# Second FFN down stage: seven half-size products per batch of blocks in place of eight, with six running sums on chip

## The chip, the cores and the metric

The kernel runs on one core of one Trainium2 chip. The metric is the device time of one execution in microseconds (us). A time from a profile is from one profiled execution; its span goes from the first to the last instruction.

The engines are called as in the profile: PE is TensorE (matmul), PEld its weight loads, DVE is VectorE, ACT is ScalarE, POOL is GpSimd, and SP is SyncE, which here only issues DMAs.

## The reference

One layer of a hybrid encoder: chunked attention and an RWKV-7 time mix, gated and merged, and then a feed-forward part. All is float32. The change touches only the second matrix product of the feed-forward part and what follows it:

```python
D_MODEL = 1024; SEQ = 2048; D_FF = 4096
...
hf = rms_norm(x, pre_ffn_g[l])
u = jnp.square(jax.nn.relu(hf @ w_up[l])) @ w_down[l]
x = x + rms_norm(u, post_ffn_g[l])
```

The stage in question computes `u` and the last line for the upper half of the sequence, 1024 tokens: a product of 1024 x 4096 by 4096 x 1024.

## The kernel before

**Precision.** Every float32 product is made of three passes on TensorE. `split` writes an operand as a high part (a cast on ScalarE to the matmul's float32 format, line 66) and a low part (source minus high part on VectorE, line 67). `mm3` (line 75) then issues high x high, high x low and low x high into the same PSUM tile.

**Order of the program.** `run` goes through four groups of 512 tokens (RWKV, attention, merge), and then through the feed-forward part in two halves of 1024 tokens: `phase_up(0)`, `phase_down(0)`, `phase_up(1)`, `phase_down(1)`. Beside `phase_down(0)` other work is interleaved; beside `phase_down(1)` there is none. The tile framework allots the buffers, sets the semaphores and orders the instructions of each engine beforehand.

**The up stage** writes the hidden activations, transposed, to DRAM: `self.ad[fb]` holds block `fb` of 128 hidden features, as 128 partitions x 2 groups x 512 tokens. There are 32 such blocks for a half. It uses the same kind of seven-product scheme already, for the first product of the feed-forward part.

**The down stage before** (`phase_down`) takes two blocks at a time. `load(fb)` fetches 128 rows of `w_down` (512 KB, `wdraw`) and the block of activations (512 KB, `araw`) through SP's queue into two of the four `raw` buffers, and splits both into a tile `fop` of 16 KB a partition; the tiles come in turn from the pool of `z` (two buffers) and a ring of two. `down` runs the products of the two blocks and adds each PSUM tile to the sums `u` of eight token tiles by 1024 columns (line 1178):

```python
for t in range(th * GT, (th + 1) * GT):
    for n in range(2):
        ps = pn.tile([P, G], F32, tag="dn", name="ps_dn")
        self.mm3(ps, [(w[:, 2, sl], w[:, 3, sl], w[:, 0, ns], w[:, 1, ns]) for w in ws])
        ...
        nc.vector.tensor_tensor(u[t][:, ns], u[t][:, ns], ps, ALU.add)
```

`pn` has four PSUM buffers. So each output tile of 128 tokens by 512 columns takes six matmuls and one eviction for each pair of blocks.

**The end.** In the last pair of blocks, `final(th)` follows the four token tiles of a group: two squares with a sum on ScalarE (line 1188), three small GpSimd operations that make the reciprocal root `r` (lines 1191, 99, 101), a product with the gain on VectorE (line 1193), two scaled adds with the residual `x1r` (line 1196) and the DMA to the output (line 1199). The closing work of the first group runs beside the products of the second.

**Memory.** The pools of the up stage (`ht`, `up`, `ops`) stand on the left of the on-chip memory, those of the down stage partly on the right in the same place. A tile that reuses memory waits for the last user of the tile that was there. `raw` (four buffers of 4 KB a partition), `z` (two of 16 KB), the pool `b` (tags `bh` and `bl`, 16 KB each) and PSUM stay allotted over both stages.

Of the kernel before, what the change touches and what calls it, by code (L numbers as in the profile page):

```python
# [8 lines left out]
F32 = mybir.dt.float32  # L9
BF16 = mybir.dt.bfloat16  # L10
F32R = mybir.dt.float32r
AF = mybir.ActivationFunctionType
ALU = mybir.AluOpType
# [4 lines left out]
P = 128  # L18
D = 1024
KB = D // P  # L20
FF = 4096
HW = 512
NP = 4
G = 512
GT = G // P
# [3 lines left out]
RMS_EPS = 1e-6  # L29
# [12 lines left out]
def advance(steps, n=None):  # L42

    while n is None or n > 0:
        if next(steps, steps) is steps:
            return
        n = n and n - 1


class Block:  # L50
# [1091 lines left out]
    def phase_down(self, half, zp, rp, cb, pn, beside_of):  # L1142
# [4 lines left out]
        with ExitStack() as ctx:  # L1147
# [63 lines left out]
                        advance(beside, 1)  # L1211
            advance(beside)


    def run(self):
        tc, e = self.tc, None
        with ExitStack() as ctx, ExitStack() as mixing:
            e = mixing.enter_context
            consts = self.constants(ctx, mixing)
            advance(consts, 1)  # L1220
            self.pd = ctx.enter_context(tc.tile_pool(name="pd", bufs=2, space=PSUM))
            self.wp = e(tc.tile_pool(name="w", bufs=2))
            self.hp = e(tc.tile_pool(name="h", bufs=1))
            with tc.tile_pool(name="p0", bufs=2, reuse_waits="tile") as sp, \
                 tc.tile_pool(name="p0p", bufs=2, space=PSUM, reuse_waits="tile") as pt:
                advance(self.phase_norm(0, sp, pt, GT))
            advance(consts)
            self.order, self.next = [], None
            for g in range(self.NG):
                self.g = g  # L1230
                self.phase_rwkv(g)
                self.phase_attention(g)
                with ExitStack() as c:
                    early = iter(())
                    if g == self.NG - 1:
                        early = self.combinations(0, c.enter_context(tc.tile_pool(name="p1", bufs=1, reuse_waits="tile")), 2)
                    sp = c.enter_context(tc.tile_pool(name="p0", bufs=2, reuse_waits="tile"))
                    pt = c.enter_context(tc.tile_pool(name="p0p", bufs=2, space=PSUM, reuse_waits="tile"))
                    o = [sp.tile([P, D], F32, tag="o", bufs=GT, name=f"o{t}") for t in range(GT)]
                    self.phase_merge(g, o, self.after(g, sp, pt), early)  # L1240
                    for t in range(GT):
                        self.nc.scalar.dma_start(self.od[g][t], o[t])
            mixing.close()
            e = ctx.enter_context
            zp = e(tc.tile_pool(name="z", bufs=2, reuse_waits="tile"))
            bp = e(tc.tile_pool(name="b", bufs=1, reuse_waits="tile"))
            rp = e(tc.tile_pool(name="raw", bufs=4, side="right", reuse_waits="tile"))
            cb = e(tc.tile_pool(name="cb", bufs=3, side="right", reuse_waits="tile"))
            pn = e(tc.tile_pool(name="ffpd", bufs=4, space=PSUM, reuse_waits="tile"))

            def beside(op, pt):
                for g in (2, 3):
                    yield from self.residuals(g, op, pt, 1)
                yield from self.combinations(1, op)
                yield from self.first_half(2, bp)

            advance(self.first_half(0, bp))
            self.phase_up(0, zp, rp, cb, pn, 8)
            self.phase_down(0, zp, rp, cb, pn, beside)
            self.phase_up(1, zp, rp, cb, pn, 8)  # L1260
            self.phase_down(1, zp, rp, cb, pn, lambda op, pt: iter(()))


_INS = [
# [35 lines left out]
```

## Time and profile before

| what | value |
|---|---|
| median of 3 runs | 3430.61 us (3426.16 to 3436.8) |
| the profiled execution | 3436.05 us |
| its span | 3434.4 us |
| mean granted TensorE clock | 0.988 |
| busy: PE, DVE, ACT, POOL | 96%, 70%, 41%, 12% of the span |
| 3120 to 3200 us: PE, DVE, ACT, POOL busy | 80.00, 53.12, 12.90, 0.00 us |
| 3120 to 3200 us: DMA | 0.29 of 16 engines, 92 GB/s |

A row of the timeline gives start and duration in us, engine, line, operation, output <- inputs, shapes and the number of instructions merged (x2); where an engine sat idle before it, the idle time and what ended it stand in brackets. A row of the groups gives the sum of the busy time and the mean in ns, and then the idle time of the engine just before them. A row of windows gives, for each engine, busy time and instructions in a stretch, then the granted clock, the DMA share and GB/s. A row of the chain gives start, time, engine and line of one link of the work that ended last.

### The profile page before, as it was taken

To read this page: it belongs to the slowest core of one execution; us is meant where nothing else is said; L and a number is where in the kernel's file an instruction comes from. 1 tells how busy PE (TensorE), PEld (TensorE's weight loads), DVE (VectorE), ACT (ScalarE), POOL (GpSimd) and SP (SyncE) were. 2 spreads that over 40 slices of the span, in tenths; PEclk is the share of its full clock that TensorE was granted. 3 is DMA by queue.
4 is the path that set the end of the run, shared out by engine and by line. 5 is a ranking of instruction groups with operands and counts; after the bars stand their busy time and mean duration, and the time that the engine had idled before them with its cause. 6 is when DMAs were issued, how large, how long until landed. Compare 5 with 4: busy or idle time off the path is not lost. (4 is left out here: it accounts for less than half of the span.)

```text
span 3434.4 us, 50373 instructions
## 1 busy us (share of the span) xinstructions
PE 3297.5 (96%) x19233; PEld 2674.4 (78%) x19233; DVE 2412.8 (70%) x4110; ACT 1414.1 (41%) x2319; POOL 419.6 (12%) x796
## 2 busy tenths in 40 slices
PE   7999999999989999989999989999999999999998
PEld 5777777777867777867777877888888878888886
DVE  5774856766865766865775865877887788676667
ACT  4434634436644435644445634333321243331112
POOL 2210002101022111012210000111200021100001
PEclk9999999999999999999999999999999999999999
DMA  5224353225373125373224276434845374343333
GB/s 146 84 82 130 130 191 113 63 90 191 113 270 123 59 87 181 120 264 123 72 88 143 90 267 217 132 117 148 297 152 182 95 241 135 117 144 98 98 98 110
DMA packets 397864, 481.10 MB, mean 140 GB/s; under 512 B 17516, under 2 KB 304432, under 8 KB 397624
## 3 DMA queue, kind: packets, MB, share of 16 engines
q1 hardware_dynamic: 346168, 364.63, 34.1%
q0 software_dynamic: 23040, 79.71, 6.1%
q10 hardware_dynamic: 28416, 33.56, 2.9%
q8 instruction: 151, 2.47, 0.3%
q14 instruction: 89, 0.73, 0.1%
HBM read 356.16 MB, written 124.81 MB: 140 GB/s over the span
## 5 line engine op out<-in xcount | busy, mean ns | idle before, releaser
L75 PE MATMUL ps_dn<-fop 128*128 128x512 f32 x3072 | 702.6, 390 | 4.1 <-DVE u L1178 4.1
L75 PEld LDWEIGHTS ps_dn<-fop 128*128 128x128 f32 x3072 | 576.7, 188 | 126.2 <-DVE u L1178 6.0
L75 PE MATMUL psd<-hh,whi 128*128 128x512 f32 x1344 | 542.8, 404 | 8.0 <-ACT whi L66 7.1
L75 PE MATMUL psd<-hl,whi 128*128 128x512 f32 x1344 | 541.7, 403 | 0.0
L75 PE MATMUL psd<-hh,wlo 128*128 128x512 f32 x1344 | 538.4, 401 | 0.6 <-DVE wlo L67 0.5
L66 ACT CAST whi<-wraw 128x1024 fp32r<-128x1024 f32 x232 | 243.2, 1049 | 516.9 <-PE psd L75 405.8
L1178 DVE TENSOR_TENSOR u<-u,ps_dn 128x512 f32<-128x512 f32 x480 | 323.3, 685 | 149.5 <-PE ps_dn L75 148.7
L67 DVE TENSOR_TENSOR wlo<-wraw,whi 128x1024 fp32r<-128x1024 f32 x232 | 282.9, 1220 | 199.1 <-ACT whi L66 180.9
L75 PEld LDWEIGHTS psd<-hh,whi 128*128 128x128 f32 x1344 | 256.9, 191 | 60.9 <-ACT whi L66 7.9
L75 PEld LDWEIGHTS psd<-hh,wlo 128*128 128x128 f32 x1344 | 256.5, 191 | 50.5 <-DVE wlo L67 2.0
L75 PEld LDWEIGHTS psd<-hl,whi 128*128 128x128 f32 x1344 | 256.8, 191 | 50.0
L66 ACT CAST fop<-wdraw 128x1024 fp32r<-128x1024 f32 x64 | 67.0, 1047 | 427.4 <-PE ps_dn L75 236.0
L1099 POOL DMA_DIRECT2D ad<-r x128 | 69.2, 541 | 586.3 <-DVE r L1098 570.2
L968 PE MATMUL ps_o<-whi,mh 128*128 128x512 f32 x256 | 103.4, 411 | 16.6 <-ACT whi L66 12.3
L75 PE MATMUL ps_p<-yh,whi 128*128 128x512 f32 x256 | 103.8, 405 | 14.6 <-DVE th L939 12.7
L66 ACT CAST s12h<-s 128x1024 fp32r<-128x1024 f32 x32 | 33.7, 1054 | 184.6 <-PE ps_u L75 184.6
L831 DVE CUSTOM_DVE_ANT_0 sc<-bias,ps_s 128x640 f32<-128x640 f32 (+4 forms) x128 | 93.4, 730 | 22.3 <-PE ps_pt L843 18.1
L836 ACT ACTIVATE sc<-sc,mn 128x640 f32<-128x640 f32 (+4 forms) x128 | 97.7, 764 | 19.3 <-DVE mn L831 18.5
L75 PE MATMUL ps_p<-yh,wlo 128*128 128x512 f32 x256 | 104.2, 408 | 0.1
L847 ACT CAST PTh<-ps_pt 128x640 fp32r<-128x640 f32 (+4 forms) x128 | 80.0, 625 | 58.7 <-PE ps_pt L843 57.6
L75 PE MATMUL ps_p<-yl,whi 128*128 128x512 f32 x256 | 103.5, 404 | 0.0
L1097 ACT ACTIVATE r<-r 128x512 f32<-128x512 f32 x128 | 80.7, 630 | 54.2 <-DVE r L1096 54.0
(352 smaller groups left out, 6668.2 us busy)
## 6 DMA issues: line engine op xcount, KB each, us to landing
wraw<-in_w_in_dram SPq DMA_DIRECT2D x168, 512.0 KB
wraw<-in_w_up_dram SPq DMA_DIRECT2D x80, 512.0 KB
ad<-r POOLq DMA_DIRECT2D x128, 256.0 KB, 2.4
wdraw<-in_w_down_dram SPq DMA_DIRECT2D x64, 512.0 KB
araw<-ad SPq DMA_DIRECT2D x64, 512.0 KB
gd<-gate ACTq DMA_DIRECT2D x64, 256.0 KB
th<-gd SPq DMA_DIRECT2D x32, 512.0 KB
wraw<-in_w_out_dram SPq DMA_DIRECT2D x32, 512.0 KB
```

Of the source, the lines that this page charges most:

```text
L66: self.nc.scalar.copy(hi, src)
L67: self.nc.vector.tensor_tensor(lo, src, hi.bitcast(F32), ALU.subtract)
L75: mm = nc.tensor.matmul(ps, l, r, start=n == 0, stop=n == last).ins
L831: nc.vector.tensor_tensor_reduce(sc[:, 0:n], bias[:, s0:640], pss[:, c0 : c0 + n], 1.0, 3.0e38, ALU.add, ALU.min, mn,)
L836: nc.scalar.activation(sc[:, 0:n], sc[:, 0:n], AF.Exp, scale=-1.0, bias=mn, accum_out=sm)
L847: nc.scalar.copy(hv, pst[:, 0:nk])
L968: nc.tensor.matmul(ps[t], l[:, k, ts], r[:, k % 2], start=k == 0 and j == 0, stop=k == KB - 1 and j == 2)
L1097: nc.scalar.activation(r, r, AF.Relu)
L1099: nc.gpsimd.dma_start(self.ad[fb][:, th], r)
L1178: nc.vector.tensor_tensor(u[t][:, ns], u[t][:, ns], ps, ALU.add)
```

## The change

The second call of `phase_down` is replaced by a new function, `phase_down_fast`. The rest of the kernel stays.

**The products.** The 1024 x 4096 by 4096 x 1024 product is taken as 16 pairs of blocks. With the tokens in two groups, the columns in two halves, and the two blocks of a pair as the inner halves, it is a product of 2 x 2 quarters: a11, a12, a21, a22 by b11, b12, b21, b22. Seven products of combined quarters make the four output quarters in place of eight: the operands of step 1 are a11 and b11, of step 2 a12 and b21, of step 3 a sum of quarters `s` and b22, of step 4 a22 and a sum `t`, of steps 5 and 6 earlier values of `s` and `t`, and of step 7 the differences a11 - a21 and b22 - b12.

**Batches.** The 16 pairs go in batches of 2, 4, 4, 4 and 2. Within a batch a product of step `m` sums over all its pairs in PSUM: 4 token tiles of 128, each 3 matmuls a pair. Its tiles are then added to running sums that live through all batches: four output quarters `y`, and `xs` and `v7`, which several outputs share. In the first batch the sums begin with a copy on ScalarE where they are new; in the last batch `xs` and `v7` are added to the outputs, and `final(th, t)` follows each tile of steps 2 and 4. The order of the steps is 5, 6, 3, 4, 7, 1, 2, with other orders in the first and the last batch.

**Operands.** `operands(b, m)` makes the combinations of a step, on VectorE for `t` in steps 5 and 6 and on GpSimd for the others, in pieces of 128 x 1024, and splits both operands piece by piece. It is called for the next step before `product` of the present one. In a full batch a step takes one `z` buffer and one of `bh` and `bl`; in a batch of two a step takes one of these four.

**Loads.** Eight quarters have one buffer each, 8 KB a partition, on the right side (`fdq`). `fetch` loads quarters of the next batch after the step that used the present ones last; `free` lists which ones after which step. A piece of an activation quarter comes by two DMAs of 256 KB, a piece of a weight quarter by one of 512 KB, all by SP. The first batch has its first four quarters in the `raw` buffers and the others in halves of four of the eight buffers; from the second batch on, `s` and `t` take the `raw` buffers.

The diff, without its empty lines:

```diff
--- before.py
+++ after.py
@@ -1211,6 +1211,202 @@
                         advance(beside, 1)
             advance(beside)
 
+    def phase_down_fast(self, half, zp, bp, rp, cb, pn):
+        tc, nc, a = self.tc, self.nc, self.a
+        H = D // 2
+        gs = (2 * half, 2 * half + 1)
+        batches, at = [], 0
+        for x in (2, 4, 4, 4, 2):
+            batches.append((at, x))
+            at += x
+        assert at == FF // P // 2
+        end = len(batches) - 1
+        order = [(5, 6, 3, 4, 7, 1, 2)] * len(batches)
+        order[0], order[end] = (2, 1, 5, 6, 7, 4, 3), (5, 6, 3, 1, 2, 7, 4)
+        factors = {1: ("a11", "b11"), 2: ("a12", "b21"), 3: ("s", "b22"), 4: ("a22", "t"),
+                   5: ("s", "t"), 6: ("s", "t"), 7: ("a21", "b12")}
+        free = [{7: ("a11",), 4: ("b21",), 3: ("b22", "a12")}]
+        free += [{4: ("a22",), 7: ("a21", "b12", "b22"), 1: ("b11", "a11"), 2: ("a12", "b21")}] * end
+        with ExitStack() as ctx:
+            e = ctx.enter_context
+            cp = e(tc.tile_pool(name="fdu", bufs=1, reuse_waits="tile"))
+            qp = e(tc.tile_pool(name="fdq", bufs=1, side="right", reuse_waits="tile"))
+            y = [cp.tile([P, GT, D], F32, name=f"y{i}") for i in range(2)]
+            xs = cp.tile([P, GT, H], F32, name="xs")
+            v7 = cp.tile([P, GT, H], F32, name="v7")
+            lo, hi = slice(0, H), slice(H, D)
+            Q = {}
+            def quarter(tag):
+                return qp.tile([P, 4, H], F32, tag=tag, name="q" + tag)
+            def pair():
+                return rp.tile([P, D], F32, tag="raw", name="wdraw").rearrange("p (i n) -> p i n", i=2)
+            def load(b, q, pieces):
+                i0, x = batches[b]
+                r, c = int(q[1]) - 1, int(q[2]) - 1
+                Q[b, q] = pieces
+                for j, t in enumerate(pieces):
+                    i = i0 + 2 * j
+                    if q[0] == "a":
+                        for k in range(2):
+                            nc.sync.dma_start(t[:, k], self.ad[2 * (i + k) + c][:, r])
+                    else:
+                        rows = a["w_down"][2 * i * P : (2 * i + 4) * P, c * H : (c + 1) * H]
+                        nc.sync.dma_start(t, rows.rearrange("(i c p) n -> c p i n", c=2, p=P)[r])
+            def fetch(b, qs):
+                for q in qs:
+                    t = quarter(q)
+                    load(b, q, [t[:, j : j + 2] for j in range(0, batches[b][1], 2)])
+            for q in ("a12", "b21", "a11", "b11"):
+                load(0, q, [pair()])
+            home = {q: quarter(q) for q in ("a12", "b21", "a11", "b22")}
+            for q, t in (("a22", "a12"), ("a21", "b21"), ("b12", "a11"), ("b22", "b22")):
+                load(0, q, [home[t][:, 0:2]])
+            Q[0, "s"], Q[0, "t"] = [home["a12"][:, 2:4]], [home["b21"][:, 2:4]]
+            fetch(1, ("a21", "a22", "b12", "b11"))
+            def combine(eng, b, o, x, op, z):
+                for t, u, v in zip(Q[b, o], Q[b, x], Q[b, z]):
+                    eng.tensor_tensor(t, u, v, op)
+            made = []
+            def operands(b, m):
+                x = batches[b][1]
+                if (b, "s") not in Q:
+                    Q[b, "s"], Q[b, "t"] = ([pair() for _ in range(0, x, 2)] for _ in range(2))
+                if m == 5:
+                    combine(nc.gpsimd, b, "s", "a21", ALU.add, "a22")
+                    combine(nc.vector, b, "t", "b12", ALU.subtract, "b11")
+                elif m == 6:
+                    combine(nc.gpsimd, b, "s", "s", ALU.subtract, "a11")
+                    combine(nc.vector, b, "t", "b22", ALU.subtract, "t")
+                elif m == 7:
+                    combine(nc.gpsimd, b, "a21", "a11", ALU.subtract, "a21")
+                    combine(nc.gpsimd, b, "b12", "b22", ALU.subtract, "b12")
+                i = len(made)
+                if x == 4:
+                    t = [zp.tile([P, 4, D], F32R, tag="z", name="fop").rearrange("p f (i n) -> p (f i) n", i=2),
+                         bp.tile([P, KB, G], F32R, tag="b" + "hl"[i % 2], name="fop2")]
+                elif i % 4 < 2:
+                    t = [zp.tile([P, 4, D], F32R, tag="z", name="fop").rearrange("p f (i n) -> p (f i) n", i=2)]
+                else:
+                    t = [bp.tile([P, KB, G], F32R, tag="b" + "hl"[i % 2], name="fop2")]
+                f = []
+                for n, q in enumerate(factors[m]):
+                    dst = t[n] if x == 4 else t[0][:, 4 * n : 4 * n + 4]
+                    h, l = dst[:, 0:x], dst[:, x : 2 * x]
+                    f.append((h, l))
+                for j in range(0, x, 2):
+                    for (h, l), q in zip(f, factors[m]):
+                        self.split(h[:, j : j + 2], l[:, j : j + 2], Q[b, q][j // 2])
+                if m == 6:
+                    combine(nc.gpsimd, b, "s", "a12", ALU.subtract, "s")
+                    combine(nc.gpsimd, b, "t", "b21", ALU.subtract, "t")
+                made.append(f)
+            def keep(dst, ps, new):
+                if new:
+                    nc.scalar.copy(dst, ps)
+                else:
+                    nc.vector.tensor_tensor(dst, dst, ps, ALU.add)
+            def product(b, m, f):
+                x = batches[b][1]
+                (ah, al), (bh, bl) = f
+                add = lambda o, z: nc.vector.tensor_tensor(o, o, z, ALU.add)
+                for t in range(GT):
+                    ts = slice(t * P, (t + 1) * P)
+                    ps = pn.tile([P, G], F32, tag="dn", name="ps_dn")
+                    self.mm3(ps, [(ah[:, i, ts], al[:, i, ts], bh[:, i], bl[:, i]) for i in range(x)])
+                    c11, c12, c21, c22 = (y[r][:, t, s] for r in range(2) for s in (lo, hi))
+                    new, last = b == 0, b == end
+                    if m == 1:
+                        keep(c11, ps, False)
+                        keep(xs[:, t], ps, new)
+                        if last:
+                            add(c12, xs[:, t])
+                            add(v7[:, t], xs[:, t])
+                    elif m == 2:
+                        keep(c11, ps, new)
+                    elif m == 3:
+                        keep(c12, ps, new)
+                    elif m == 4:
+                        keep(c21, ps, new)
+                    elif m == 5:
+                        keep(c22, ps, new)
+                        if last:
+                            add(c12, c22)
+                    elif m == 6:
+                        keep(xs[:, t], ps, False)
+                    else:
+                        keep(v7[:, t], ps, new)
+                        if last:
+                            add(c22, v7[:, t])
+                            add(c21, v7[:, t])
+                    if last and m in (2, 4):
+                        final(m // 2 - 1, t)
+            X = {}
+            def inputs(th, tags):
+                for k, tag in enumerate(tags):
+                    x = quarter(tag).rearrange("p (t i) n -> p t (i n)", t=2)
+                    for j in range(2):
+                        t = 2 * k + j
+                        nc.sync.dma_start(x[:, j], self.x1[gs[th]][t * P : (t + 1) * P])
+                        X[th, t] = x[:, j]
+            def final(th, t):
+                g, u = gs[th], y[th][:, t]
+                ssq = cp.tile([P, 2], F32, tag="ssq", bufs=4, name="ssqu")
+                for n in range(2):
+                    sq = cb.tile([P, G], F32, tag="c", name="squ")
+                    nc.scalar.activation(sq, u[:, n * H : (n + 1) * H], AF.Square, accum_out=ssq[:, n : n + 1])
+                nc.gpsimd.tensor_tensor(ssq[:, 0:1], ssq[:, 0:1], ssq[:, 1:2], ALU.add)
+                r = self.rstd(cp, ssq[:, 0:1], 1.0 / D, RMS_EPS)
+                nc.vector.tensor_tensor(u, u, X["g"], ALU.mult)
+                for n in range(2):
+                    ns = slice(n * H, (n + 1) * H)
+                    nc.vector.scalar_tensor_tensor(
+                        u[:, ns], u[:, ns], r, X[th, t][:, ns], op0=ALU.mult, op1=ALU.add
+                    )
+                nc.sync.dma_start(self.out[g * G + t * P : g * G + (t + 1) * P], u)
+            steps = [(b, m) for b in range(len(batches)) for m in order[b]]
+            operands(*steps[0])
+            for i, (b, m) in enumerate(steps):
+                if i + 1 < len(steps):
+                    b1, m1 = steps[i + 1]
+                    operands(b1, m1)
+                    if b1 < end:
+                        fetch(b1 + 1, free[b1].get(m1, ()))
+                    elif m1 == 1:
+                        inputs(0, ("b11",))
+                    elif m1 == 2:
+                        X["g"] = quarter("b21").rearrange("p (t i) n -> p t (i n)", t=2)[:, 0]
+                        nc.sync.dma_start(X["g"], a["post_ffn_g"][None, :].to_broadcast((P, D)))
+                        x = quarter("a12").rearrange("p (t i) n -> p t (i n)", t=2)
+                        for j in range(2):
+                            nc.sync.dma_start(x[:, j], self.x1[gs[0]][(2 + j) * P : (3 + j) * P])
+                            X[0, 2 + j] = x[:, j]
+                    elif m1 == 7:
+                        inputs(1, ("a11", "b22"))
+                product(b, m, made[i])
 
     def run(self):
         tc, e = self.tc, None
@@ -1258,7 +1454,7 @@
             self.phase_up(0, zp, rp, cb, pn, 8)
             self.phase_down(0, zp, rp, cb, pn, beside)
             self.phase_up(1, zp, rp, cb, pn, 8)
-            self.phase_down(1, zp, rp, cb, pn, lambda op, pt: iter(()))
+            self.phase_down_fast(1, zp, bp, rp, cb, pn)
 
 
 _INS = [
```

## The prediction

> **What bounds the kernel now.** I read the page's busy shares first, then the chain of waits to its end, then the busy time by windows inside the second down stage, then the groups of that stage, and last the timeline of single instructions for the prices.
>
> ```profile
> PE 3297.5 (96%) x19233; PEld 2674.4 (78%) x19233; DVE 2412.8 (70%) x4110; ACT 1414.1 (41%) x2319; POOL 419.6 (12%) x796
> 3068.73 337.71 PE ps_dn L75 x1488
> 3429.26 0.75 DVE u L1196
> 3430.02 0.66 DVEq L1296
> 3200.00:3280.00 80.00, 80.00 (x354) 66.18 (x353) 56.47 (x76) 14.40 (x15) 0.00 (x0) 1.00 0.35 106
> 3400.00:3434.00 34.00, 17.60 (x77) 13.92 (x75) 28.07 (x38) 9.70 (x28) 14.17 (x24) 0.85 0.61 216
> ```
>
> The chain shows the stage that is replaced: it starts at 3068.73 us and 1488 matmuls follow on TensorE without a gap. The window row has TensorE busy for all 80 us, VectorE for 56.5, GpSimd for none. So the body of the stage is TensorE's; the last 34 us are VectorE's (28.07 busy against 17.60). From 3068.73 to the end of the span (3434.4) are 365.7 us, and only these can change. One matmul costs 337.71 / 1488 = 0.227 us.
>
> ```profile
> L1178 DVE TENSOR_TENSOR u<-u,ps_dn 128x512 f32<-128x512 f32 x240 | 162.6, 686 | 96.4 <-PE ps_dn L75 96.3
> L67 DVE TENSOR_TENSOR fop<-araw,fop 128x1024 fp32r<-128x1024 f32 x32 | 39.0, 1220 | 0.0
> L66 ACT CAST fop<-araw 128x1024 fp32r<-128x1024 f32 x32 | 33.5, 1047 | 1.1 <-DMA araw<-ad 1.0
> 3411.99 1.88 DVE L1178 TENSOR_TENSOR u<-u,ps_dn 128x512 f32<-128x512 f32 x3
> 3420.80 2.35 DVE L1193 TENSOR_TENSOR u<-u,g_post 128x1024 f32<-128x1024 f32 x2
> 3423.07 1.41 DVE L1196 SCALAR_TENSOR_TENSOR u<-u,rs_r,x1r 128x512 f32<-128x512 f32 x2
> ```
>
> These are VectorE's prices. A row that merges instructions shows that those back to back overlap: three evictions take 1.88 us, so the second and third cost 0.60 each, not 0.69; the second 128x1024 one costs 2.35 - 1.22 = 1.13, and a scaled add 0.66.
>
> **What TensorE saves.** Before, the stage has 32 blocks x 16 output tiles x 3 = 1536 matmuls. After, each of 16 pairs of blocks has 7 products x 4 tiles x 3 = 84, in all 1344. The 192 removed are worth 192 x 0.227 = 43.6 us. A product of a batch of four takes 48 x 0.227 = 10.9 us, such a batch 76.3; a batch of two 24 matmuls a product, 38.1. The batches are 2, 4, 4, 4, 2.
>
> **What VectorE gets.** A full batch has 28 splits (7 products, 2 operands, 2 pieces of 128x1024), 4 combinations for t in steps 5 and 6, and 32 evictions (product 1 goes to two sums). That is 32 x 1.13 + 32 x 0.60 = 55.4 us back to back, or 32 x 1.22 + 32 x 0.69 = 61 by the single durations. Before, the same eight blocks had 16 splits and 64 evictions, 18.1 + 38.4 = 56.5 us in 87 of TensorE. So VectorE has as much to do in 76 us: it still fits. ScalarE's 28 casts of 1.05 fit too.
>
> **What GpSimd gets, and the port.** Step 5 adds two pieces for s, step 6 subtracts two before its split and four after it, and step 7 makes four: 12 pieces of 128x1024 a full batch. No such instruction is in this stage before. The nearest rows come from the RWKV stage, a pair of 128x512 with two inputs in SBUF:
>
> ```profile
> 171.45 2.05 POOL L399 TENSOR_TENSOR mN<-mI,n 128x512 f32<-128x512 f32 x2
> 171.94 0.69 DVE L607 TENSOR_TENSOR S<-ps_s,gC 128x512 f32<-128x512 f32 x1 [1.50 <-PE ps_s L606]
> 103.51 3.00 POOL L399 TENSOR_TENSOR mN<-mI,n 128x512 f32<-128x512 f32 x2
> 104.05 1.54 DVE L429 TENSOR_TENSOR BK<-tk,Ei 64x512 f32<-64x512 f32 x1
> 105.61 1.44 DVE L432 SCALAR_TENSOR_TENSOR r<-r,cst,tk 128x512 f32<-128x512 f32 x1
> 67.23 0.68 DVE L429 TENSOR_TENSOR BK<-tk,Ei 64x512 f32<-64x512 f32 x1
> 67.92 0.75 DVE L432 SCALAR_TENSOR_TENSOR r<-r,cst,tk 128x512 f32<-128x512 f32 x1
> ```
>
> At 171 us the pair takes 2.05 us, and the VectorE instruction beside it, with one input in PSUM, its usual 0.69. At 103 us the pair takes 3.00, and the two VectorE instructions beside it, both inputs in SBUF, take 1.54 and 1.44 where the same lines take 0.68 and 0.75 elsewhere. So the two engines take turns when both read two inputs from SBUF, and don't when VectorE evicts PSUM. I price a piece of 128x1024 at the pair's 2.05 us: 24.6 us a full batch. The Trainium skill's page "GPSIMD Engine Reference", Elementwise — side-by-side cycle accounting, gives 4497 ns for 2048 columns, so by estimate 2.25 for 1024; with that the sum below would be some 4 us longer. No run here shows that size.
>
> A GpSimd piece thus costs VectorE up to 2.05 us, less the 0.60 of an eviction that fits beside it: 1.45. The operands of a step can be split only while the product ahead of it runs, since each step takes one z and one b buffer of two. I go through these windows of 10.9 us, in the order 5, 6, 3, 4, 7, 1, 2:
> - While product 5 runs, step 6 is made: first cast 1.05, two combinations and four splits at about 1.17 (7.0), two evictions between them 1.2, and the first two later pieces for s taking turns, 2 x 1.45 = 2.9. Together 12.2: 1.3 late.
> - While product 6 runs, step 3 needs four splits, each of which takes turns with a piece (two for t, then those of step 7): 4 x (2.05 + 1.22) = 13.1, 2.2 late.
> - Steps 4, 7, 1 and 2 have four splits and four to eight evictions, 7.1 to 9.5 us, and at most two more pieces: they fit, as does step 5, whose s can be made a window earlier.
>
> So a full batch loses 3.5 us. The ends are 0 (all pieces fall on evictions or idle time) and 61 + 24.6 - 76.3 = 9.3 (no overlap at all). I take 3.5, nearer to the rows, which show evictions untouched.
>
> **The start.** The first two products read from the four raw buffers, free before the up stage ends, and their splits go to z buffers that nobody else holds. The loads of the other quarters go to memory of the up stage's tiles.
>
> ```profile
> SPq L110 <- PE ps_u L75: 11.1, 1, 11.1
> 3424.90 4.25 DMA x1r<-x
> 2776.00:2793.00 17.00, 15.51 (x68) 12.20 (x67) 11.89 (x13) 12.70 (x16) 1.08 (x2) 1.00 1.02 380
> 3052.50 0.59 ACT L1130 COPY p<-ps_u 128x512 f32<-128x512 f32 x1 [1.38 <-PE ps_u L75]
> ```
>
> The issue for the gain's tile, in that same memory before, waited 11.1 us for the up stage's TensorE work. I take the home loads as issued at about 3069; the first 512 KB land some 4 us later (x1r took 4.25) and the others at up to 380 GB/s, so a22, a21 and b12 are there at 3075 to 3077. A GpSimd piece, a cast and two splits later step 5 is ready at about 3081, against 3079.6 when products 2 and 1 are done; step 7, with three pieces in its way, may lose one more. I take 2.5 us (0 to 8). Six of the eight evictions of a tile go to ScalarE here (0.59 each), so VectorE has room.
>
> **The last batch.** Here VectorE is the bound: 32 evictions 19.2, 14 splits 15.8, two combinations 2.3, 20 adds between sums at an eviction's price 12.0, and the closing work on eight rows, 8 x (1.13 + 2 x 0.66) = 19.6: 68.9 us against 38.1 of TensorE. Both closing passes, that of the upper rows too, now lie on this path. From the end of the batch before: 68.9, less 4.5 done earlier (step 5 and t of step 6), plus 0.6 for the last eviction, 2.9 for two GpSimd pieces, 2 for the squares and rstd of the last row, and 3.7 from the last scaled add (3430.7) to the end: 73.6. The ends are 70 (no idle time, no turns) and 84 (single durations, 76.9, two full pieces and 4 idle).
>
> **The sum.** 38.1 + 2.5 + 3 x (76.3 + 3.5) + 73.6 = 353.6 us in place of 365.7: 12.1 less. Of the 43.6 saved on TensorE, about 18 go into the last batch, where the old stage overlapped closing work with products, 10.5 into the port's turns and 2.5 into the start. The profiled run took 3436.05 us (span 3434.4), 5.4 above the median of the runs, so I set the difference against the median: 3430.6 - 12.1 = 3418.5. A measurement of this kernel can tell about 0.3%, 10.3 us.
>
> **The rivals.**
> - **The port costs nothing.** The pieces fall where VectorE idles or evicts, full batches take 76.3 and the last part 70: 337 us in all, 3402. For it: VectorE needs only 55.4 of 76.3. Against it: the pieces cluster in four of seven steps. Chance 0.15.
> - **The shared port becomes the bound (slower).** No piece overlaps an eviction, because the order on VectorE's queue is fixed beforehand and an eviction stands behind a waiting split: full batches take 85.6, the last part 84, in all 38.1 + 2.5 + 256.8 + 84.4 = 381.8, that is 16.1 more, 3446.7. With a last part of 80 it decides for slower from about 8.8 us lost in a full batch. For it: the rows at 103 us, where both engines lose; against it: evictions ran beside GpSimd unhurt. Chance 0.27. The Trainium skill has this rule in "SBUF — State Buffer", Who interferes with whom: a VectorE instruction with two SBUF inputs and a GpSimd one that reads SBUF hold the read port in turn, for the whole instruction. The trace agrees (1.54 against 0.68 us).
> - **Loads come late.** The next batch's b11 is issued once step 1 has split the old one, behind 3 MB of a21, b12 and b22. At 380 GB/s that lands in time; at half of it b11 comes at about the start of product 2, where it is needed. 3 us at each of four batch changes give 12 us, 3430.5: no difference. Chance 0.10.
> - **The clock drops in the last batch.** TensorE would be busy for 38 of 74 us there; the window from 3400, busy for 52%, has a granted clock of 0.85. If it falls to half, the 38.1 us of products become 76 and pass VectorE's 68.9 by 7: 3426. Chance 0.06.
>
> **How the numbers follow.** My forecast has 0.42, with an own range of 3408 to 3430; about 0.26 of that is faster by over 0.3% (under 3420.3), 0.16 within it. With the rivals: faster 0.26 + 0.15 = 0.41; within 0.3% 0.16 + 0.10 + 0.06 = 0.32; slower 0.27. The range runs from the first rival, 3402, to all bounds at their upper end, 38.1 + 8 + 256.8 + 84.4 = 387.3, 3452.
>
> **What would show it.** 1344 matmuls of the stage at 0.227 us; some 112 splits and 136 PSUM adds on VectorE; 48 GpSimd pieces near 2.05 us or, where they took turns, up to 3.3; splits with a mean above 1.22 us. TensorE's waits should be for VectorE's splits in steps 6 and 3 of each full batch, near 3.5 us a batch, and in the last batch for evictions. It would be wrong if GpSimd's pieces cost far from 2 us, if full batches wait for DMA, or if VectorE idles for over 5 us in the last batch.

## The result and the profile after

The changed kernel takes 3445.05 us (median of 6 runs, 3441.2 to 3447.84) against 3429.7 before: a ratio of 1.0042, 95% interval 1.0032 to 1.0052. It is slower, by about 15 us, where I forecast 12 less; 3445 lies outside my own range of 3408 to 3430 and near the rival of the shared port (3446.7).

The replaced stage begins at 3068.57 us in the profile shown of before and at 3062.76 in that of after, though nothing ahead of it was changed. So I compare stages, from the first matmul of the down stage to the end of the span: 365.8 us before, 380.9 after. Three rows of windows of after cut it at the first matmul of the full batches (3115.13) and at that of the last batch (3369.74):

```profile
3062.76:3115.13 52.37, 43.34 (x169) 34.27 (x167) 46.26 (x29) 26.54 (x37) 39.61 (x15) 0.90 0.56 198
3115.13:3369.74 254.61, 236.33 (x1009) 193.22 (x1010) 216.08 (x190) 81.51 (x85) 98.29 (x34) 0.97 0.25 84
3369.74:3440.10 70.36, 44.43 (x169) 33.91 (x167) 67.79 (x88) 20.86 (x43) 24.08 (x26) 0.85 0.29 111
```

TensorE is no longer busy all the time: of 254.6 us in the three full batches it misses 18.3, and the granted clock is 0.97 there and 0.90 in the first batch. GpSimd, idle in the body of this stage before, works for 98.3 us in the full batches and 39.6 in the first. Start, full batches and end take 52.4, 254.6 and 74.0 us (to 3443.7); the forecast had 40.6, 239.4 and 73.6. So of the 27.3 us that the stage is over the forecast, 15.2 lie in the full batches and 11.8 in the start.

The groups of after, from the beginning of the stage to the end, have the splits at 1.6 to 1.9 us, where the same line took 1.22 before, and GpSimd's pieces at 2.7 to 3.3:

```profile
L67 DVE TENSOR_TENSOR fop<-wdraw,fop 128x1024 fp32r<-128x1024 f32 x42 | 79.6, 1928 | 1.3 <-ACT fop L66 1.3
L67 DVE TENSOR_TENSOR fop<-qa,fop 128x1024 fp32r<-128x1024 f32 x33 | 54.7, 1661 | 3.6 <-ACT fop L66 3.5
L67 DVE TENSOR_TENSOR fop<-qb,fop 128x1024 fp32r<-128x1024 f32 x33 | 52.5, 1593 | 0.0
L1281 POOL TENSOR_TENSOR wdraw<-qa,wdraw 128x1024 f32<-128x1024 f32 x7 | 23.3, 3337 | 18.4 <-DVE fop L67 18.4
L1281 POOL TENSOR_TENSOR qb<-qb,qb 128x1024 f32<-128x1024 f32 x7 | 19.7, 2810 | 8.5 <-PE ps_dn L75 4.7 <-ACT fop L66 3.8
L1281 POOL TENSOR_TENSOR wdraw<-qa,qa 128x1024 f32<-128x1024 f32 x7 | 18.7, 2675 | 81.5 <-DMA qa<-ad 81.1 <-issue 0.4
```

If two engines take turns at 1.2 and 2.4 us, an instruction of either can last up to 3.6 us with its wait; the longest here last 3.3 to 3.4. How it stops TensorE is seen in the timeline of one place, the end of the second batch, which is the first full one (`qa` and `qb` are the quarters, `wdraw` the buffers of `s` and `t`, line 1281 the combinations, 1324 the evictions):

```profile
3174.92 2.40 POOL L1281 TENSOR_TENSOR qa<-qa,qa 128x1024 f32<-128x1024 f32 x1 [7.51 <-DMA qa<-ad]
3178.62 2.41 POOL L1281 TENSOR_TENSOR qb<-qb,qb 128x1024 f32<-128x1024 f32 x1 [1.31 <-ACT fop L66]
3180.99 3.37 POOL L1281 TENSOR_TENSOR qa<-qa,qa 128x1024 f32<-128x1024 f32 x1
3184.32 3.35 POOL L1281 TENSOR_TENSOR qb<-qb,qb 128x1024 f32<-128x1024 f32 x1
3179.00 3.11 DVE L1281 TENSOR_TENSOR wdraw<-qb,qb 128x1024 f32<-128x1024 f32 x1
3182.03 3.41 DVE L67 TENSOR_TENSOR fop<-qa,fop 128x1024 fp32r<-128x1024 f32 x1
3185.36 3.39 DVE L67 TENSOR_TENSOR fop<-qb,fop 128x1024 fp32r<-128x1024 f32 x1
3188.68 1.21 DVE L67 TENSOR_TENSOR fop<-qa,fop 128x1024 fp32r<-128x1024 f32 x1
3190.95 0.68 DVE L1324 TENSOR_TENSOR y<-y,ps_dn 128x512 f32<-128x512 f32 x1
3192.37 24.49 PE L75 MATMUL ps_dn<-fop,fop 128*128 128x512 f32 x96 [6.13 <-DVE xs L1324]
```

GpSimd makes the differences of step 7 for the next batch, as soon as its quarters have landed, while VectorE splits the operands of step 2. Each of three VectorE instructions takes 3.1 to 3.4 us in place of 1.21; as soon as GpSimd is through, one takes 1.21 again. The evictions of product 1 stand behind all four splits, and TensorE, which needs a free PSUM buffer for product 2, waits 6.13 us. The same happens a batch later (6.21 us). And the 96 matmuls after the gap take 24.49 us where 96 x 0.227 is 21.8 (a batch later 23.98); the last two rows are from there:

```profile
3192.30:3196.00 3.70, 3.63 (x9) 2.92 (x10) 3.70 (x7) 0.00 (x0) 0.00 (x0) 0.50 0.87 293
3196.00:3200.00 4.00, 4.00 (x16) 3.21 (x15) 4.00 (x3) 0.00 (x0) 2.97 (x1) 0.80 0.42 163
3200.00:3204.00 4.00, 4.00 (x19) 3.31 (x18) 4.00 (x5) 0.00 (x0) 2.84 (x2) 1.00 0.00 0
3278.80:3283.00 4.20, 4.18 (x10) 3.33 (x11) 4.20 (x7) 0.00 (x0) 0.00 (x0) 0.50 0.94 308
3283.00:3287.00 4.00, 4.00 (x19) 3.26 (x19) 4.00 (x3) 0.00 (x0) 3.31 (x1) 1.00 0.27 102
```

After the first gap the granted clock is half for some 5 us (0.50, then a mean of 0.80), after the second for some 4. The two gaps and the slower matmuls behind them make 17 of the 25.9 us by which the full batches exceed the 228.7 of the kernel without combinations below. The Trainium skill's page "TensorE: Matmul & The Clock Gate", Part 1, says that an idle window of about 3.4 us halves the clock and that as much work brings it back. Both gaps here are longer than that and halved it, and the way back took somewhat longer than stated. But in the kernel with all combinations on VectorE, below, a gap of 2.48 us was already enough (a clock of 0.51 from 3122 to 3124 us), while one of 2.15 was not (1.00 behind it).

### The profile page after: what moved, and what is told of

It reads as the page before. It is cut to its first block, busy times and chain, and to the rows that moved or that the text cites. A ratio compares the mean times of both kernels' runs of the same rounds, so it can differ in the third digit from the quotient of the medians.

```text
span 3443.7 us, 49967 instructions
## 1 busy us (share of the span) xinstructions
PE 3270.0 (95%) x19041; PEld 2647.0 (77%) x19041; DVE 2485.8 (72%) x4074; ACT 1472.2 (43%) x2391; POOL 566.7 (16%) x844
## 5 line engine op out<-in xcount | busy, mean ns | idle before, releaser
L75 PE MATMUL ps_dn<-fop 128*128 128x512 f32 x1872 | 441.0, 397 | 25.3 <-DVE v L1324 8.5
L75 PEld LDWEIGHTS ps_dn<-fop 128*128 128x128 f32 x1872 | 357.0, 192 | 105.4 <-issue 12.8
L75 PE MATMUL ps_dn<-fop,fop 128*128 128x512 f32 x1008 | 236.5, 397 | 20.0 <-DVE xs L1324 12.3
L75 PEld LDWEIGHTS ps_dn<-fop,fop 128*128 128x128 f32 x1008 | 193.0, 192 | 63.5 <-issue 14.6
L66 ACT CAST fop<-wdraw 128x1024 fp32r<-128x1024 f32 x78 | 80.2, 1047 | 279.7 <-PE ps_dn L75 118.1
L1178 DVE TENSOR_TENSOR u<-u,ps_dn 128x512 f32<-128x512 f32 x240 | 160.6, 685 | 51.5 <-PE ps_dn L75 51.1
L67 DVE TENSOR_TENSOR fop<-wdraw,fop 128x1024 fp32r<-128x1024 f32 x78 | 123.6, 1602 | 6.9 <-ACT fop L66 6.8
```

What stands on the lines that cost most here:

```text
L66: self.nc.scalar.copy(hi, src)
L67: self.nc.vector.tensor_tensor(lo, src, hi.bitcast(F32), ALU.subtract)
L75: mm = nc.tensor.matmul(ps, l, r, start=n == 0, stop=n == last).ins
```

## The experiments

The theory after the result, A: what costs the time is that GpSimd's combinations and VectorE's instructions with two inputs in SBUF take turns. B: the loads come late. C: VectorE has too much to do, whoever combines. All kernels below are the changed kernel with the edit shown. Stage times are worked out as above, each from one profiled execution (the expectation that counts 49.4 us to the full batches begins at a matmul 3 us after the first one); "ratio" is to the kernel before.

| kernel | start | full batches | end | stage | median, ratio (interval) |
|---|---|---|---|---|---|
| before | | | | 365.8 | |
| changed | 52.4 | 254.6 | 74.0 | 380.9 | 1.0042 (1.0032 to 1.0052) |
| no combinations | 38.8 | 228.7 | 70.3 | 337.8 | one run: 3408.21 us |
| fills in their place | 39.0 | 228.5 | 71.7 | 339.2 | one run: 3409.16 us |
| no loads from batch 3 | 52.5 | 240.4 | 75.0 | 367.9 | one run: 3431.89 us |
| all on VectorE | 41.2 | 237.4 | 73.6 | 352.2 | 3423.46, 0.9973 (0.9962 to 0.9984) |
| step 7 on VectorE | 47.6 | 246.9 | 74.4 | 368.9 | 3435.81, 1.0006 (0.9997 to 1.0015) |
| products first | 56.2 | 246.8 | 74.5 | 377.5 | 3448.84, 1.0049 (1.0033 to 1.0065) |
| all on VectorE, products first | 42.3 | 229.1 | 73.0 | 344.4 | 3412.06, 0.9938 (0.9925 to 0.9951) |

**Without combinations.**

```diff
-                    combine(nc.gpsimd, b, "s", "a21", ALU.add, "a22")
+                    for t, u in zip(Q[b, "s"], Q[b, "a21"]):
+                        nc.scalar.copy(t, u)
...
-                    combine(nc.gpsimd, b, "s", "s", ALU.subtract, "a11")
```

(The other four calls go likewise.)

> The GpSimd combinations are left out (s is a copy of a21 by ScalarE, the others keep what the buffers hold), so the output is not the reference's; matmuls, splits, evictions and loads stay. In the changed kernel the stage takes 49.4 us to the first matmul of the full batches, 254.6 for the three full batches and 74.0 from there to the end. Theory A (GpSimd and VectorE take turns at the read port): splits fall from 1.6 to 1.9 us to 1.22, the full batches to 229 to 234, the start to 40 to 44, the end to 68 to 71; the span falls by 28 to 38 us. Theory B (loads come late): the full batches stay near 250. Theory C (VectorE simply has too much to do, whoever combines): VectorE's own instructions are the same, so the full batches stay near 250.

The full batches take 228.7 us, the 76.3 of TensorE alone three times; the start 38.8, the end 70.3. The splits of this kernel:

```profile
L67 DVE TENSOR_TENSOR fop<-wdraw,fop 128x1024 fp32r<-128x1024 f32 x42 | 49.8, 1218 | 5.4 <-ACT fop L66 5.4
```

VectorE's own instructions, the loads and the matmuls were the same, so B and C fall as first causes, and A stands, for the start as for the full batches. What goes too is every wait for a result of GpSimd's; the next kernel keeps those.

**Fills in place of combinations.**

```diff
-                    combine(nc.gpsimd, b, "s", "a21", ALU.add, "a22")
+                    write(b, "s", "a21", ALU.add, "a22")
...
+            def write(b, o, *_):
+                for t in Q[b, o]:
+                    nc.gpsimd.memset(t, 0.5)
+                    nc.gpsimd.memset(t, 1.0)
```

(The other five calls go likewise.)

> Each GpSimd combination is replaced by two fills of the same piece, which write and read nothing (the output is not the reference's). Theory A, if the turns are over reading: splits at 1.22 us and the full batches as without combinations, 229 to 236. If GpSimd blocks VectorE also when it only writes: splits stay at 1.5 us or more and the full batches above 243.

```profile
L67 DVE TENSOR_TENSOR fop<-wdraw,fop 128x1024 fp32r<-128x1024 f32 x42 | 49.9, 1219 | 6.7 <-ACT fop L66 6.4
L1286 POOL MEMSET wdraw<- 128x1024 f32 x26 | 24.7, 953 | 1.3
L1285 POOL MEMSET wdraw<- 128x1024 f32 x26 | 24.7, 953 | 66.7 <-DVE fop L67 66.7
```

GpSimd is busy at the same points of the program, 1.9 us a piece, and nothing is slowed: 228.5 us. A fill is shorter than an addition (1.9 against 2.4 us), so waits for GpSimd's results shrink as well; but in the changed kernel casts wait for these only 6.6 us in all three full batches, too little for the loss. So it is GpSimd's reading that holds VectorE up, not that it works or writes (an instruction of one input was not tried). That is the Trainium skill's rule in "SBUF — State Buffer", Who interferes with whom, that a GpSimd instruction which only writes does not contend with a VectorE instruction of two SBUF inputs; this run agrees.

**Without the later loads.**

```diff
                 for q in qs:
+                    if b > 1:
+                        Q[b, q] = Q[1, q][: batches[b][1] // 2]
+                        continue
                     t = quarter(q)
```

> The loads of batches 3 to 5 are left out; they use again what the buffers hold from batch 2 (the output is not the reference's). GpSimd's combinations stay. Theory B: the full batches fall from 254.6 to 229 to 236. Theory A: they stay at 248 to 260, with splits at 1.6 us or more.

Neither theory had it: 240.4 us. The turns stay; the splits of `s` and `t` take even more, but TensorE waits less, for no gap is over 1.7 us after the first products of the second batch (evictions are line 1327 here):

```profile
L67 DVE TENSOR_TENSOR fop<-wdraw,fop 128x1024 fp32r<-128x1024 f32 x42 | 83.3, 2014 | 1.6 <-ACT fop L66 1.5
3210.11 11.13 PE L75 MATMUL ps_dn<-fop,fop 128*128 128x512 f32 x48 [1.66 <-DVE y L1327]
3288.93 51.28 PE L75 MATMUL ps_dn<-fop,fop 128*128 128x512 f32 x222 [1.67 <-DVE y L1327]
```

Of the 25.9 us that the full batches lose, 14 hang on when the pieces run: GpSimd waits 81.1 us for `qa` in the changed kernel, and then runs step 7's pieces beside the splits of the old batch's step 2. Here it runs them one after another at 3235 to 3247 us, inside their own batch, and TensorE does not stop there. The loads are not late for TensorE (without combinations they cost nothing); they set when GpSimd's work falls. With the loads gone the order fixed on the queues may differ too, so that the landing alone does it is not shown, and the share is a rough one.

**All combinations on VectorE.**

```diff
-                    combine(nc.gpsimd, b, "s", "a21", ALU.add, "a22")
+                    combine(nc.vector, b, "s", "a21", ALU.add, "a22")
```

(The other five calls go likewise.)

> All combinations on VectorE, none on GpSimd; everything is computed. A full batch then has 44 instructions of 1.13 us and 32 evictions of 0.60, 69 us of VectorE in 76.3 of TensorE. Theory A: splits at 1.22 us, full batches 231 to 240 in place of 254.6, start 42 to 46, end 75 to 79; span 15 to 28 us shorter than that of the changed kernel, and 5 to 18 shorter than before. Theory C: VectorE gets 54 us more, so it is slower than the changed kernel by 10 to 40 us. Theory B: as the changed kernel, within 5 us.

Faster than the changed kernel and than before, 0.9973, as A said. VectorE got 48 more instructions and yet the stage is 28.7 us shorter. A piece costs VectorE 1.13 to 1.22 us if it makes it itself. On GpSimd it cost VectorE more by waiting: the recorded splits of the changed kernel sum to 186.8 us for 108, at 1.22 each 131.8, so 55 us too long, and its combinations for `t` another 11; 66 us for 48 pieces are 1.4 each.

**Step 7 alone on VectorE.**

```diff
-                    combine(nc.gpsimd, b, "a21", "a11", ALU.subtract, "a21")
-                    combine(nc.gpsimd, b, "b12", "b22", ALU.subtract, "b12")
+                    combine(nc.vector, b, "a21", "a11", ALU.subtract, "a21")
+                    combine(nc.vector, b, "b12", "b22", ALU.subtract, "b12")
```

> Only the four pieces of step 7 move from GpSimd to VectorE (eight a full batch stay on GpSimd); everything is computed. In the changed kernel these four come when a11 and b22 have landed, beside the splits of step 5 at the batch change, where TensorE then waits 6.1 and 6.2 us for an eviction. Theory A1 (the loss sits where the loads make the pieces pile up on splits): those waits go, full batches 236 to 243 in place of 254.6. Theory A2 (every piece costs about the same, wherever it runs): 8/12 of the loss of 25.8 stays, full batches 244 to 248. Theory C (VectorE has too much work): it gets 4.5 us more a batch, full batches 255 or more.

246.9 us, as A2: 18.2 of the 25.9 us lost stay, 70% with two thirds of the pieces. (The expectation puts the step 7 pieces beside the splits of step 5; the timeline above shows them beside `t` of step 5 and the splits of step 2.) The waits ahead of product 2 are gone, as A1 had it, but two products later, between products 5 and 6 of the next batch, where the changed kernel waits 1.06 and 1.56 us, TensorE now waits 4.73 and 5.18:

```profile
3211.77 28.47 PE L75 MATMUL ps_dn<-fop,fop 128*128 128x512 f32 x114 [4.73 <-DVE y L1324]
```

Again the evictions stand behind four splits, those of step 6, which take 9 us beside later pieces of `s` and `t`. So no single bunch is the cause: with 12 pieces or 8 a batch, those that fall on splits stop TensorE. (VectorE's four added pieces have a part in it: with all of them on VectorE the waits at this place are 2.48 and 1.91 us for evictions and 2.15 for a cast.)

**Products ahead of the next operands.**

```diff
+                if b < end:
+                    product(b, m, made[i])
                 if i + 1 < len(steps):
                     b1, m1 = steps[i + 1]
...
-                product(b, m, made[i])
+                if b == end:
+                    product(b, m, made[i])
```

> The changed kernel, all on GpSimd as there, but up to the last batch the product of a step is written ahead of the operands of the next, so that on VectorE's queue a ready eviction goes ahead of splits. In the changed kernel four splits stand in a row, each waiting for a GpSimd piece, and the four evictions come behind them. Theory A3 (what stops TensorE is the eviction behind waiting splits; one eviction hides beside a GpSimd piece): waits for evictions go, full batches 236 to 244 in place of 254.6, the span 8 to 18 us shorter. Theory A4 (the window is simply too short for pieces and splits, whatever the order): TensorE waits for splits in place of evictions, full batches 250 to 260.

Between the two: the full batches fall to 246.8, the start rises to 56.2, and by the runs nothing is gained (1.0049 against 1.0042, the intervals overlap). Why the start rose stays open. The gap at product 2 turns into one for splits:

```profile
3192.97 47.23 PE L75 MATMUL ps_dn<-fop,fop 128*128 128x512 f32 x200 [4.01 <-DVE fop L67]
```

So the eviction behind the splits is a part of it; without it the splits themselves are late.

**The same order with all combinations on VectorE.** (The last edit and that of all combinations on VectorE together.)

> The same order with all combinations on VectorE. Nothing waits for a port, so the order matters less: full batches 230 to 238 against 237.4 with splits first; the span 0 to 7 us shorter than with splits first.

229.1 us for the full batches, better than expected, and no wait of TensorE's in them. Its windows, cut as for the changed kernel:

```profile
3063.70:3106.04 42.34, 39.84 (x170) 31.25 (x169) 37.79 (x38) 27.46 (x39) 0.93 (x2) 1.00 0.69 246
3106.04:3335.14 229.10, 228.97 (x1009) 189.13 (x1008) 208.26 (x227) 81.67 (x84) 0.00 (x0) 1.00 0.28 94
3335.14:3404.40 69.26, 44.25 (x169) 33.89 (x167) 66.85 (x90) 20.86 (x43) 17.85 (x24) 0.85 0.30 110
```

The clock is 1.00 until the last batch. At 0.9938 of before (0.9925 to 0.9951) this has the lowest median of the kernels that compute everything, 21 us under the kernel before: the seven products are worth their price once GpSimd is out of the way.

**A last batch of four.** Three kernels with batches of 2, 2, 4, 4, 4: one with all on VectorE, one with GpSimd as in the changed kernel, and the first of these with products first:

```diff
-        for x in (2, 4, 4, 4, 2):
+        for x in (2, 2, 4, 4, 4):
```

> As the kernel with all combinations on VectorE, with batches of 2, 2, 4, 4, 4 in place of 2, 4, 4, 4, 2; everything is computed. The closing work (adds between sums 12 us, closing of eight rows 19.6) then lies beside 76 us of TensorE in place of 38. VectorE in the last batch: 69 + 31.6 = 100.6 us against 76.3; in the second batch of two 44 against 38.1. From the first matmul of the stage: 41 + 44 to 46 + 2 x 79 + 101 to 106 = 344 to 351 us, against 352.2 with the old batches and 365.8 before. If the closing work is not bound by VectorE's sum but by its chain of waits, nothing is gained: 352 or more.

> The changed kernel with its combinations on GpSimd, and batches of 2, 2, 4, 4, 4; everything is computed. By the port's turns the two batches of two at the start lose 14 us and some 8 more, the full batches 8.6 each, and the last batch is bound by VectorE at 101 us plus about 15 for turns: stage 370 to 385 us, against 380.9 in the changed kernel. If the order of the batches alone made the loss, it falls to that of the kernel with combinations on VectorE, 344 to 351.

> The same order with all combinations on VectorE and batches of 2, 2, 4, 4, 4. In that kernel without the new order TensorE waits 4.8, 3.3, 3.9 and 3.7 us for evictions at the batch changes and 5.5 in the last batch. If the new order takes the first four away, the stage falls from 353.7 to 338 to 346 us; if they turn into waits for splits, 350 to 356.

All on VectorE takes 353.7 us for the stage (ratio 0.9952, 0.9939 to 0.9966), with products first 347.1 (0.9957, 0.9945 to 0.9969), on GpSimd 377.4 (one run, 3447.58 us), as the turns would have it. By the stage nothing is gained on VectorE (352.2 and 344.4 with the old batches). By the runs the first is a little under the old batches (0.9952 against 0.9973, the intervals just overlap) and the second not (0.9957 against 0.9938). In the first, the two full batches and the last took 269.5 us together, where I had 259 to 264: the last some 104, as expected, and the full ones some 83 each in place of 79, with waits of 3.3 and 3.9 us for evictions. At the first of them these stand behind four splits and four combinations on VectorE's queue (3154 to 3163 us). So the last batch took what the sum said, and the time went into the others.

## Why the prediction was wrong, point by point

- **TensorE's saving** held. Without combinations the full batches take 228.7 us, the 3 x 76.3 of the sum.
- **VectorE's own work** held: 55.4 us a full batch by the sum; without combinations VectorE is busy for 165.51 us in the three (55.2 each).
- **The price of a GpSimd piece** was too low: 2.40 us undisturbed, not 2.05 from the pair of 128x512; the estimate of 2.25 from the Trainium skill's page was nearer.
- **The price of a turn to VectorE**, 1.45 us a piece, was about right on the whole (1.4 measured), but that is luck, for its make-up was wrong. It was a piece less one eviction beside it. Evictions do run beside a piece unhurt (four in 2.47 us at 3217.10 in the changed kernel, a piece from 3216.06 to 3219.44), but at the batch change they stand behind the splits on VectorE's queue, as the rival had it, and a split that takes its turn lasts 3.4 us.
- **"They fit, as does step 5" is the step that failed.** I laid the pieces over the windows by the order of the steps. In the changed kernel they run after the quarters have landed, in bunches, above all those of the next batch's step 7 beside the splits of step 2. That window, which I counted as free, costs 6.1 and 6.2 us, and I had 3.5 a batch in other windows. A full batch lost 8.6 us. Without the later loads, with step 7's pieces inside their own batch, it lost 3.9. The sign that I named, TensorE's waits for splits in steps 6 and 3, came to 1.0 us in the three full batches; 12.3 are the waits for evictions of product 1.
- **The clock.** I had it only as a rival for the last batch. It fell after gaps in the full batches: of the 25.9 us lost there, 18.3 are idle TensorE and 7.6 slower matmuls (236.3 us busy against 228.7).
- **The start**, 2.5 us (0 to 8), lost 14.3, outside its bounds: a second step that failed, and nearly as dear as the first. I had weighed the loads, one piece ahead of step 5 and three ahead of step 7; the loads were issued from 3057.5 us, 5 us ahead of the stage rather than at its beginning, and were not what was late. GpSimd is busy for 39.6 of 52.4 us, with seven pieces nearly in a row at its beginning, two of them for the next batch. Casts wait for it up to 3.9 us, and TensorE's longest wait, 4.45 us, is for splits that take 3.3 us each. Without its combinations the start takes 38.8. A step lasts 5.4 us here and a piece 2.4 to 3.4; how much is GpSimd's own time and how much the turns, no run separates.
- **The last batch**, 73.6 us, came out at 74.0, and bound by VectorE as forecast (67.8 us busy of 70.4). The 18 us or so of the saving that the sum put there stayed there.

The rival of the shared port had the right sign, the right mechanism and nearly the time (3446.7). That it came so near is luck: it put 84.4 us into the end and 40.6 into the start, where 74.0 and 52.4 were measured, and the two errors cancel; in a full batch it had 9.3 where 8.6 were lost. I held evictions beside GpSimd for evidence against it; that row said that they can run there, not that they would.

## What to carry to other kernels

Before giving elementwise work to GpSimd, see whether VectorE reads two SBUF inputs in the same stretch: here each piece cost VectorE 1.4 us of waiting, more than the 1.2 of making it. Lay such pieces out in time by when their inputs land, not by the order of the program, and ask what stands behind a blocked instruction on its queue. A gap on TensorE can cost more than itself: after the two of some 6 us the next 96 matmuls took 2.7 and 2.2 us longer.

## What was not expected of the hardware

The turns were in the forecast; their size and their limit were not. GpSimd filling 128x1024 (0.95 us) slows VectorE by nothing, while an addition of the same size holds a split for over 2 us. Both engines lose by the turns: a piece takes 3.3 in place of 2.4 us, a split 3.4 in place of 1.2. And the clock, which I had doubted only for the last batch, halved after gaps of 6.13, 6.21 and once of 2.48 us.
